# A running sum of squares on VectorE: fewer sums over the partitions in thirteen norms

## The chip, the cores and the metric

The kernel runs on one core of a Trainium2 chip. The metric is the device time of one launch in microseconds (us). TensorE is called PE here, VectorE DVE and ScalarE ACT, as in the profile; SP issues the loads.

## The reference

256 tokens of width 1024 go through two blocks of two layers each. The first block has a gated linear attention layer and a sliding-window attention layer, each followed by a product-key expert layer (PEER); the second has an mLSTM layer and a latent attention layer (MLA), each followed by a squared-ReLU FFN. Every sublayer starts from an RMS norm, and in the second block its output is normed too before it is added:

```python
def rms_norm(x, g):
    xf = x.astype(jnp.float32)
    y = xf * lax.rsqrt(jnp.mean(xf * xf, axis=-1, keepdims=True) + EPS)
    return (y * g.astype(jnp.float32)).astype(x.dtype)

def modulate_2(h, shift, scale):
    return h * (1 + scale[:, None, :]) + shift[:, None, :]
...
        h = modulate_2(rms_norm(x, norm_g[layer, 0]), sh1, sc1)
        ...
        x = x + g1[:, None, :] * rms_norm(y, norm_g[layer, 1])
        h = modulate_2(rms_norm(x, norm_g[layer, 2]), sh2, sc2)
        y = sq_relu_mlp(h, ffn_w1[layer], ffn_w2[layer])
        x = x + g2[:, None, :] * rms_norm(y, norm_g[layer, 3])
```

What matters here is the mean of squares over the 1024 columns of each token.

## The kernel before

Activations lie transposed: the 1024 columns are eight tiles of 128 partitions, and the 256 tokens lie along the free dimension. A sum over the columns is therefore a sum over eight tiles and over the partitions of each. ACT squares a tile (`Stats.add`); DVE adds two squares (`Stats.pairs`); and PE sums over the partitions by a matmul with a matrix of ones, which accumulates in one PSUM region and leaves the sum on every partition (`Stats.sums`). ACT then makes the reciprocal root as Ln and Exp (`rstd`, lines 422 and 423).

Before, the squares of tiles 0 and 1, 2 and 3, 4 and 5 are added in pairs, and tiles 6 and 7 stand alone: five sums. `pairs(2)` is called behind every odd tile and takes up squares that lie at least two tiles back, so the pair (0, 1) is added after tile 3, (2, 3) after tile 5, (4, 5) after tile 7. `total` gives out first the sums that are ready, in their order, then takes up the rest.

The weights come as a stream of chunks of 128x1024 in fp32. Each is split by ACT into a high part (`whi`, line 304) and by DVE into the rest (`wlo`, line 312), and every product is made of three matmuls in fp32r: high by high, high by low, low by high. The order of the instructions on each engine is written out by hand (`manual_schedule`); semaphores follow from the tiles.

Thirteen norms have eight tiles, and they stand in four kinds of places:

- one at the very start (`rstd` of the first stage);
- five in `add_gated`, at the end of the two attention layers and the two PEER layers of the first block: as each pair of accumulators is finished, DVE updates two tiles of x, ACT makes the high part of the next matmul's operand (`xah`) and the square, DVE the low part (`xal`). The last of these places makes two norms at once, the second with a tag of its own and five buffers instead of six;
- four in `add_sandwich`, at the end of each sublayer of the second block: the squares are those of the accumulators; once the sums are done, `ry` is made, and y, x and the next operand follow from it (`fold`, `refresh`);
- three in `fold`, on the x that `refresh` makes two tiles at a time.

For the gated norms and the folds the sums are not made at once: the next stage's first matmuls (`first_linears`, on the operand before the norm's factor, which is applied later) run over the tiles as they come, and PE is given the sums ahead of its last chunk. There are also a norm over two tiles and one over three, both in the MLA layer.

Of the kernel before, what the change touches and what calls it, by code (L numbers as in the profile page):

```python
# [277 lines left out]
class Stream:  # L278
# [4 lines left out]
    def __init__(self, k, dram):  # L283
        self.k, self.nc, self.dram = k, k.nc, dram
        self.off = [0]
        for w in WIDTHS:
            self.off.append(self.off[-1] + 128 * w)
        self.raw, self.hi, self.lo = {}, {}, {}
        self.nd = self.nh = self.nl = self.at = 0
# [84 lines left out]
class Stats:  # L374


    def __init__(self, k, pool, dim, n, dst=None, tag="", ss=None, bufs=6):
        self.bufs = bufs
        self.k, self.pool, self.dim, self.n, self.dst, self.tag = k, pool, dim, n, dst, tag
        self.seen, self.squares, self.ready, self.first = 0, deque(), deque(), ss is None  # L380
        self.ss = k.pw([128, T]) if ss is None else ss
# [7 lines left out]
    def pairs(self, lag=0):  # L389

        while self.squares and self.squares[0][0] + lag < self.seen:
            i, q = self.squares[0]
            if i % 2 == 0 and i + 2 < self.n:
                if i + 1 + lag >= self.seen:
                    return
                self.squares.popleft()
                i, p = self.squares[0]
                self.k.nc.vector.tensor_add(p, p, q)
                q = p
            self.squares.popleft()  # L400
            self.ready.append((i, q))

    def sums(self):
# [1617 lines left out]
```

## Time and profile before

| | before |
|---|---|
| median of 3 runs | 2526.88 us (2524.39 to 2527.84) |
| profiled execution | 2536.26 us, span 2534.5 us |
| PE busy | 2463.7 us (97%) |
| DVE busy | 2093.1 us (83%) |
| ACT busy | 1608.4 us (63%) |
| mean granted clock of PE | 0.993 |

The span runs from the first to the last instruction of the profiled execution. Busy shares are means over the whole span; a place where an engine waits is only seen in the timeline around it.

### The profile page before, as it was taken

What the parts mean: (1) busy time and instruction counts of PE and PEld (TensorE: products, weight loads), DVE (VectorE), ACT (ScalarE), POOL (GpSimd) and SP (SyncE); (2) the same over time, 40 slices, a digit from 0 to 9 for tenths busy, and PEclk for the clock granted to TensorE, in tenths of its full rate; (3) what the DMA queues carried; (4) which work ended last, traced back from release to release, by engine and by line L of the source; (5) the groups of instructions that cost most, each with busy time, mean ns of one, the idle gap of its engine ahead of it and who ended that gap; (6) DMA issues with size and microseconds to landing.
All of it is one profiled execution on the core that took longest, in us unless ns stands there. A gap on an engine that the chain in (4) does not pass through costs nothing.

```text
span 2534.5 us, 52041 instructions
## 1 busy us (share of the span) xinstructions
PE 2463.7 (97%) x20262; PEld 2407.0 (95%) x20262; DVE 2093.1 (83%) x4203; ACT 1608.4 (63%) x3208; POOL 12.4 (0%) x21
## 2 busy tenths in 40 slices
PE   8899999999999999999999999999999999989998
PEld 6799999999999998899999999999998899989998
DVE  8889988998788888699989997787887776786754
ACT  5664459997555545764469996444447666567654
POOL 0000000000000000000000000000000000000000
PEclk9999999999999999999999999999999999999999
DMA  8755554444888884245554445888885547934564
GB/s 324 269 173 184 190 184 150 150 142 148 310 300 313 316 313 161 93 151 192 188 177 144 147 145 198 305 299 301 303 306 183 195 163 262 330 135 130 159 200 142
DMA packets 149174, 537.08 MB, mean 212 GB/s; under 512 B 16560, under 2 KB 18736, under 8 KB 148928
## 3 DMA queue, kind: packets, MB, share of 16 engines
q1 hardware_dynamic: 148640, 533.23, 60.3%
q8 instruction: 159, 2.61, 0.4%
q14 instruction: 87, 0.71, 0.1%
q10 hardware_dynamic: 288, 0.52, 0.1%
HBM read 532.64 MB, written 1.05 MB: 211 GB/s over the span
## 4 chain that ended last, share of the span: by engine, by line
PE 83%; DVE 8%; ACT 5%; DMA 2%; issue 2%; SPq 0%; DVEq 0%; ACTq 0%
PE w L567 12%; PE w L569 12%; PE w L568 12%; PE acc L568 12%; PE acc L569 12%; PE acc L567 12%; PE acc L1345 4%; DVE wlo L312 3%; ACT whi L304 2%; DMA wraw<-in_weights_dram 2%; DVE mraw L650 1%; PE acc L588 1%; PE w L588 1%; PE w L406 1%; PE w L1375 1%
## 5 line engine op out<-in xcount | busy, mean ns | idle before, releaser
L304 ACT CAST whi<-wraw 128x1024 fp32r<-128x1024 f32 x785 | 818.4, 1047 | 684.1 <-PE acc L568 359.3
L312 DVE TENSOR_TENSOR wlo<-wraw,whi 128x1024 fp32r<-128x1024 f32 x785 | 955.2, 1220 | 333.3 <-ACT whi L304 319.8
L567 PE MATMUL w<-hh,whi 128*128 128x256 f32 x2664 | 759.0, 285 | 1.0 <-ACT vz L1475 0.5
L569 PE MATMUL w<-hh,wlo 128*128 128x256 f32 x2664 | 743.3, 279 | 3.1 <-DVE wlo L312 2.9
L568 PE MATMUL w<-hl,whi 128*128 128x256 f32 x2664 | 743.0, 279 | 0.0
L567 PE MATMUL acc<-Wh,whi 128*128 128x256 f32 x2048 | 570.7, 279 | 3.7 <-ACT Wh L762 3.7
L568 PE MATMUL acc<-Wl,whi 128*128 128x256 f32 x2048 | 571.2, 279 | 2.7 <-DVE Wl L763 2.6
L569 PE MATMUL acc<-Wh,wlo 128*128 128x256 f32 x2048 | 570.4, 279 | 0.0
L569 PEld LDWEIGHTS w<-hh,wlo 128*128 128x128 f32 x2664 | 506.3, 190 | 3.7 <-DVE wlo L312 3.7
L567 PEld LDWEIGHTS w<-hh,whi 128*128 128x128 f32 x2664 | 502.5, 189 | 3.6 <-ACT vz L1475 0.9
L568 PEld LDWEIGHTS w<-hl,whi 128*128 128x128 f32 x2664 | 502.2, 189 | 0.7 <-issue 0.5
L568 PEld LDWEIGHTS acc<-Wl,whi 128*128 128x128 f32 x2048 | 388.8, 190 | 3.8 <-DVE Wl L763 3.7
L567 PEld LDWEIGHTS acc<-Wh,whi 128*128 128x128 f32 x2048 | 384.4, 188 | 4.3 <-ACT Wh L762 4.3
L569 PEld LDWEIGHTS acc<-Wh,wlo 128*128 128x128 f32 x2048 | 384.4, 188 | 0.0
L650 DVE SCALAR_TENSOR_TENSOR mraw<-mraw,cact 128x1024 f32<-128x1024 f32 x224 | 272.6, 1219 | 6.6 <-DMA mraw<-in_mods_dram 4.9
L1361 ACT ACTIVATE o<-o,gT 128x128 f32<-128x128 f32 x384 | 161.1, 486 | 0.0
L567 PE MATMUL acc<-yh,whi 128*128 128x256 f32 x512 | 141.6, 277 | 0.9 <-DVE fc L849 0.9
L569 PE MATMUL acc<-yh,wlo 128*128 128x256 f32 x512 | 141.6, 277 | 0.2
L568 PE MATMUL acc<-yl,whi 128*128 128x256 f32 x512 | 141.4, 276 | 0.0
L1345 PE MATMUL acc<-o,o 128*128 128x128 f32 x1024 | 134.6, 274 | 0.0
L1357 ACT ACTIVATE o<-c_iota,iT 128x128 f32<-128x128 f32 x384 | 125.8, 400 | 0.0
L1345 PEld LDWEIGHTS acc<-o,o 128*128 128x128 f32 x1024 | 124.5, 191 | 0.0
(447 smaller groups left out, 3566.4 us busy)
## 6 DMA issues: line engine op xcount, KB each, us to landing
wraw<-in_weights_dram SPq DMA_DIRECT2D x777, 512.0 KB, 3.6
mraw<-in_mods_dram SPq DMA_DIRECT2D x224, 512.0 KB, 5.3
cact<-in_c_dram SPq DMA_DIRECT2D x5, 512.0 KB, 4.2
wraw<-in_weights_dram SPq DMA_DIRECT2D x4, 384.0 KB, 2.9
x<-in_x_dram SPq DMA_DIRECT2D x2, 512.0 KB, 4.4
wraw<-in_weights_dram SPq DMA_DIRECT2D x4, 192.0 KB, 2.4
out_dram<-x SPq DMA_DIRECT2D x2, 256.0 KB, 2.4
out_dram<-x ACTq DMA_DIRECT2D x2, 256.0 KB, 2.4
```

Source lines behind the costliest of these rows:

```text
L304: self.nc.scalar.copy(t[:, :w], self.raw[i][:, :w])
L312: self.nc.vector.tensor_sub(t[:, :w], self.raw.pop(i)[:, :w], self.hi[i][:, :w].bitcast(F32))
L406: self.k.nc.tensor.matmul(self.ss, self.k.ones, q, start=self.first, stop=i == self.n - 1, skip_group_check=True)
L567: mm(out, lh, rh, start=start, stop=False, skip_group_check=True)
L568: mm(out, lh, rl, start=False, stop=False, skip_group_check=True)
L569: mm(out, ll, rh, start=False, stop=stop, skip_group_check=True)
L588: self.nc.tensor.matmul(outs[j], ws[:, i * 128:(i + 1) * 128], xs[:, k], start=k == 0 and ws is wh and xs is x[0], stop=k == KD - 1 and xs ...
L650: self.nc.vector.scalar_tensor_tensor(t, t, 1.0, self.cact, op0=ALU.mult, op1=ALU.mult, accum_out=self.modc[:, n:n + 1])
L1345: nc.tensor.matmul(banks[(n - 1) % 4][:, u], o1[:, u], o2[:, u], start=True, stop=True)
L1357: nc.scalar.activation(o2[:, u], self.iota, AF.Abs, scale=-1.0, bias=iT[:, 1, t:t + 1])
L1361: nc.scalar.activation(o2[:, u], o2[:, u], AF.Relu, scale=gT[:, 1, t:t + 1], bias=gT[:, 0, t:t + 1])
L1375: nc.tensor.matmul(ps[:, b], q[:, b * 128:(b + 1) * 128], sk[:, i % 2], start=True, stop=True)
```

## The change

For a norm over n tiles, the squares of all but the last two tiles are added up in one running sum, each addition reading the result of the one before; the running sum is given to PE when tile n - 3 is in it. The last two squares are summed on their own, as before. The additions are called from the same places. For eight tiles that is five additions and three sums in place of three and five; for three tiles no addition and three sums, in place of one and two; for two tiles nothing changes.

```diff
     def __init__(self, k, pool, dim, n, dst=None, tag="", ss=None, bufs=6):
-        self.bufs = bufs
+        self.bufs, self.run = bufs, None
...
         while self.squares and self.squares[0][0] + lag < self.seen:
-            i, q = self.squares[0]
-            if i % 2 == 0 and i + 2 < self.n:
-                if i + 1 + lag >= self.seen:
-                    return
-                self.squares.popleft()
-                i, p = self.squares[0]
-                self.k.nc.vector.tensor_add(p, p, q)
-                q = p
-            self.squares.popleft()
+            i, q = self.squares.popleft()
+            if i < self.n - 2:
+                if self.run is not None:
+                    self.k.nc.vector.tensor_add(q, q, self.run)
+                self.run = q
+                if i < self.n - 3:
+                    continue
             self.ready.append((i, q))
```

## Rows read from the trace of the kernel before

**Rows 1.** The page: busy time and share by engine; the chain that ended last

```profile
PE 2463.7 (97%) x20262; PEld 2407.0 (95%) x20262; DVE 2093.1 (83%) x4203; ACT 1608.4 (63%) x3208; POOL 12.4 (0%) x21
...
PE 83%; DVE 8%; ACT 5%; DMA 2%; issue 2%; SPq 0%; DVEq 0%; ACTq 0%
```

**Rows 2.** Tiles of squares, by engine: count, least/median/longest ns, first and last start

```profile
L406 PE MATMUL w<-sq,ones x138: 377/379/795, 6.0 to 2524.1; 128*128 128x256 f32 x138
...
L398 DVE TENSOR_TENSOR sq<-sq x40: 417/421/430, 5.5 to 2522.4; 128x256 f32<-128x256 f32 x40
```

**Rows 3.** Timeline, first gated norm: start and length (us), engine, line, [idle before <-releaser]

```profile
152.60 0.51 ACT L461 ACTIVATE xah<-x,ua 128x256 fp32r<-128x256 f32 x1 [0.30 <-DVE x L780]
...
153.65 0.43 DVE L398 TENSOR_TENSOR sq<-sq 128x256 f32<-128x256 f32 x1
...
153.79 2.32 PE L406 MATMUL w<-sq,ones 128*128 128x256 f32 x10
...
155.17 3.50 DVE L312 TENSOR_TENSOR wlo<-wraw,whi 128x1024 fp32r<-128x1024 f32 x3 [0.62 <-ACT whi L304]
...
159.66 0.74 PE L588 MATMUL acc<-hh,whi 128*128 128x256 f32 x4 [0.29 <-ACT hh L742]
```

**Rows 4.** Timeline, first sandwich (end of the mLSTM layer)

```profile
2043.72 1.23 DVE L312 TENSOR_TENSOR wlo<-wraw,whi 128x1024 fp32r<-128x1024 f32 x1 [0.57 <-ACT whi L304]
...
2044.86 1.09 DVE L398 TENSOR_TENSOR sq<-sq 128x256 f32<-128x256 f32 x3
...
2045.43 2.40 PE L406 MATMUL w<-sq,ones 128*128 128x256 f32 x10 [0.30 <-DVE sq L398]
...
2047.86 0.47 ACT L422 ACTIVATE ry<-w,eps 128x256 f32<-128x256 f32 x1 [0.15 <-PE w L406]
...
2048.82 0.43 DVE L821 TENSOR_TENSOR y<-y,ry 128x256 f32<-128x256 f32 x1 [0.48 <-ACT ry L423]
...
2049.28 0.42 DVE L823 TENSOR_TENSOR x<-x,y 128x256 f32<-128x256 f32 x1
...
2050.30 1.01 PE L588 MATMUL w<-xah,whi 128*128 128x258 f32 x3 [2.47 <-ACT xah L461]
```

**Rows 5.** Timeline, first norm, at the start

```profile
5.99 3.87 PE L406 MATMUL w<-sq,ones 128*128 128x256 f32 x10 [5.99 <-DVE sq L398]
...
11.12 0.47 ACT L422 ACTIVATE r<-w,eps 128x256 f32<-128x256 f32 x1
```

**Rows 6.** Timeline, second sandwich (2233 to 2239) and last one (2521 to 2523)

```profile
2233.13 1.09 DVE L398 TENSOR_TENSOR sq<-sq 128x256 f32<-128x256 f32 x3
...
2233.60 2.42 PE L406 MATMUL w<-sq,ones 128*128 128x256 f32 x10 [0.89 <-DVE sq L398]
...
2238.50 0.62 PE L588 MATMUL acc<-xah,whi 128*128 128x258 f32 x3 [2.47 <-ACT xah L461]
...
2521.03 0.43 DVE L398 TENSOR_TENSOR sq<-sq 128x256 f32<-128x256 f32 x1 [4.54 <-ACT sq L385]
...
2522.18 2.32 PE L406 MATMUL w<-sq,ones 128*128 128x256 f32 x10
```

**Rows 7.** Timeline, first fold (start of the first FFN)

```profile
2059.52 0.42 DVE L398 TENSOR_TENSOR sq<-sq 128x256 f32<-128x256 f32 x1
...
2060.52 2.32 PE L406 MATMUL w<-sq,ones 128*128 128x256 f32 x10
```

**Rows 8.** Timeline, second fold (start of the MLA layer)

```profile
2246.55 2.34 PE L406 MATMUL w<-sq,ones 128*128 128x256 f32 x10
...
2246.85 0.42 DVE L398 TENSOR_TENSOR sq<-sq 128x256 f32<-128x256 f32 x1
...
2248.54 0.59 PE L588 MATMUL acc<-xah,whi 128*128 128x258 f32 x2
```

**Rows 9.** Windows after two sandwiches: busy by engine, granted clock, DMA

```profile
2050.50:2053.50 3.00, 3.00 (x15) 3.00 (x16) 2.79 (x6) 2.72 (x9) 0.00 (x0) 0.50 0.12 48
2238.50:2240.50 2.00, 2.00 (x15) 1.86 (x15) 1.97 (x5) 1.72 (x6) 0.00 (x0) 1.00 0.72 264
```

## The prediction

> **What bounds the kernel now.** I read the page first, for who is late on average, then every place where squares are summed in the timeline, because an average over 2.5 ms says nothing about 13 places of a few microseconds. The page shows TensorE (PE) busy for 97% of the span and 83% of the chain that ended last on it [rows 1]: time taken off PE is worth its full length wherever PE doesn't wait. The groups of the squares' tiles come next [rows 2]. The sums over the partitions are 138 MATMULs at one line, and one call gives two of them, so 69 calls: five for each of 13 norms over eight tiles, two for the two-tile norm, two for the three-tile norm. The 40 DVE additions are three for each of the 13 and one for the three-tile norm. Then the timeline of each place, where the reader is to ask one thing: what does PE wait for just before the sums and just after them?
>
> **What one instruction costs.** Ten sum matmuls back to back take 2.32 us, the last of them 0.38 [rows 2, 3], so their pitch is (2.32 - 0.38) / 9 = 0.216 and a call costs 0.43. Six of them run from first start to last end in 5 x 0.216 + 0.38 = 1.46. A DVE addition lasts 0.42. Three independent ones take 1.09 [rows 4], a pitch of (1.09 - 0.42) / 2 = 0.335. The new additions are not independent: each reads what the one before wrote. The nearest row of that kind is the multiply of y at 2048.82 and the addition that reads it at 2049.28, same shape and engine: a pitch of 0.46 [rows 4]. I take 0.46 for the chain and keep 0.335 as the lower end. The Trainium skill (VectorE: DVE Perf Modes, "The DRAIN you can't avoid") says that a DVE instruction starts only when the pipeline has emptied, and that a semaphore between two of them costs nothing extra; by that a chain would cost what independent additions cost, and the sum would be that of the first rival below. The rows above differ from it by 0.125 an instruction.
>
> **What the change moves.** For eight tiles five serial additions replace three independent ones, and six matmuls replace ten. Calls of `pairs` with lag 2 stay where they are: one addition after tile 3 (as now), two after tile 5 (one now), two after tile 7 (one now). The three-tile norm loses its addition and goes from two sums to three. In all PE loses 13 x 2 - 1 = 25 calls, 25 x 0.43 = 10.8 us. DVE gains 25 additions. But the order of the sums is fixed: PE takes the running sum first, and that is now the tile that is ready last of the six; before, PE had two finished pairs to chew on while DVE made the third. So each place is worked out by itself.
>
> *First norm (start).* The sums end at 9.86 (5.99 + 3.87), and its Ln starts at 11.12 [rows 5]. The first addition, 0.42 long and done just before 5.99, starts near 5.5; five chained ones end at 5.5 + 4 x 0.46 + 0.42 = 7.8, and six matmuls at the 0.39 that each of the ten takes there, waits included, end near 10.2. Hidden: 0.
>
> *Four sandwiches* (end of each mixer and FFN of the second block). PE has nothing else to do: sums, then Ln and Exp, y, x, the split, and only then PE again [rows 4]. In the first, DVE comes out of the 1.23 us `wlo` only at 2044.86. The chain ends at 2044.86 + 4 x 0.46 + 0.42 = 2047.12; PE starts 0.05 later (the gap between an addition's end, 2233.13 + 0.42, and its sum at 2233.60 [rows 6]) and ends at 2047.17 + 1.46 = 2048.63, against 2045.43 + 2.40 = 2047.83: **+0.80**. Behind the additions on DVE wait three evacuations of y, a `wlo` and a gain; they end about 0.75 later (a delay of 5 x 0.46 - 1.09 - 0.46), covered by the Ln and Exp. The second: 2233.13 + 2.26 + 0.05 + 1.46 = 2236.90 against 2233.60 + 2.42 = 2236.02: **+0.88**. The third has the first's pattern: +0.80. In the last DVE is idle, the additions start at 2521.03 while PE still accumulates, and the chain ends at 2523.29, the sums at 2524.80 against 2522.18 + 2.32 = 2524.50 [rows 6]: **+0.30**. Together +2.78, and no matmul saved there is worth anything.
>
> *Five gated norms* (in the next stage's first matmuls). PE runs through; but ACT waits for DVE's x (0.30), then come the casts, three `wlo` on DVE from 155.17 to 158.67, the normed tile, and PE waits 0.29 for it at 159.66 [rows 3]. So DVE and ACT set this stage's end, and the extra addition after tile 5 sits ahead of x of tile 6: **+0.46**. The extra one after tile 7 is hidden in DVE's wait for the casts (0.62). The 0.86 saved on PE goes into waiting: the last pair, added at 153.65, becomes a running sum at 153.65 + 0.92 + 0.42 + 0.05 = 155.04, 1.25 after PE comes for it, so PE is 0.39 later too, which the 0.46 covers. Three places: +1.38. The fourth place holds two norms at once, two extra additions ahead of the same x: +0.92. Together +2.30.
>
> *Three folds.* In the first the run of PE isn't broken and the sums stand in it. The last pair now starts at 2059.52; with one more addition after tile 5 and one after tile 7 the running sum is there at 2059.52 + 0.92 + 0.42 + 0.05 = 2060.91, 0.39 after PE comes for it at 2060.52 [rows 7]; PE then has four matmuls less: 0.39 - 0.86 = **-0.47**. The third fold has the same pattern: -0.47. In the second, three outputs bring PE to the sums earlier: 2246.55, when the last pair is only begun at 2246.85 [rows 8]. The running sum is there at 2246.85 + 0.92 + 0.47 = 2248.24; PE now takes 1.99 from the first sum to its next matmul at 2248.54, of which nine pitches are 1.94, so with six it is 5 x 0.216 + 0.03 = 1.11: 2249.35, **+0.81**. Together -0.13.
>
> *Two and three tiles.* The first unchanged; the second one sum more in PE's stream, +0.43 (the removed addition was off the path).
>
> **Sum without the clock:** 2.78 + 2.30 - 0.13 + 0.43 = **+5.4 us**.
>
> **The clock.** After the wait of 2.47 us in the first sandwich the granted clock is 0.50, that is 1.2 GHz, for the following 3 us; after the same wait of 2.47 in the second it is 1.00, 2.4 GHz [rows 6, 9], as three matmuls in 0.62 there and 1.01 here show [rows 4, 6]. So one such wait is a toss-up now. After the change each sandwich has two waits with 1.46 us of work between: some 2 us for the running sum, then 2.47 as now. The Trainium skill (TensorE: Matmul & The Clock Gate, "HAM oscillation — how this bites in real kernels") warns of this pattern, bursts between idle gaps; the trace bears it out in one of the two. Price of one more fall, from rows: 3.2 us (2050.30 to about 2053.5) at half speed, 1.6, if PE alone set the pace. If the fall comes before the sums they take 6 x 0.216 = 1.3 more, on the path, in three sandwiches 3.9. Bounds 0 and 1.6 + 3.9 = 5.5. I take 1.2, near the lower end, since the rows show a fall as likely as none after the longer of the two waits.
>
> **The forecast: +6.6 us.** The profiled execution took 2536.26 (span 2534.5 and 1.8 around it), 9.4 above the median 2526.88; I add the sum to the median: **2533.5**, own range 2530.9 to 2535.9.
>
> **Rivals.**
> *A chained addition costs what an independent one does* (0.335). For: all DVE rows back to back have that pitch; against: the y and x rows. Five additions then take 1.76 instead of 2.26: the first three sandwiches +0.30, +0.38, +0.30, the last -0.13 (there I let the last addition wait for its square, which as now comes no earlier than about 2522.4), gated 5 x 0.335 = 1.68, folds -0.72 twice and +0.56, three-tile +0.43: **+2.1**, 2529.0 without a fall of the clock.
> *The matmuls saved inside PE's stream count in full* (faster). Eight norms stand in it: 8 x 0.86 = 6.9 less, 0.43 more, sandwiches neutral: **-6.5**, 2520.4. It needs the additions hidden: DVE must have slack after tiles 5 and 7, the running sum ready before PE comes. For: DVE is idle 17% of the span [rows 1], and two folds come within 0.4 of it. Against: at the gated norms ACT and PE are seen waiting for DVE. It decides where PE's wait at 159.66 comes from: if that tile isn't held by DVE's x, the 0.46 isn't paid and the 0.86 is gained.
> *The clock falls at each longer wait:* 5.4 + 5.5 = **+10.9**, 2537.8. For: the longer idle time; against: the second sandwich.
>
> **How the numbers follow.** Forecast 0.50, cheap chain 0.22, saved matmuls 0.10, clock 0.18. 0.2% (5.05 us) is about what a measurement of this kernel can tell from no change. Slower by over that: 0.40 of the forecast's 0.50 (its range starts at +4.0) and the clock's 0.18: 0.58. Within: the other 0.10 and 0.22: 0.32. Faster 0.10. The range takes in the cheap chain and the falling clock with 0.7 for how runs differ above it, and 2.5 below the cheap chain for places where a delay is lost again: 2526.5 to 2538.5; the saved matmuls lie outside.
>
> **What would show it.** 88 sum MATMULs and 65 additions; additions after tile 7 of the first sandwich at a pitch of 0.46 (0.335 would be the cheap chain) and PE idle some 2 us before its sums, which end 0.8 later after the last accumulation than now; ACT's wait for x of tile 6 in the gated norms grown by 0.46, PE's wait of 1.25 for the running sum there, and the normed tile's matmul 0.46 later after the last accumulation; fold sums that wait for DVE; the granted clock in and after the three waits. Wrong it would be if the gated norms' next stages came no later, or if a stall is absorbed by a later wait, which would take the total under 0.2%.

## The result, and the profile after

The changed kernel took 2539.5 us in the median of 21 runs (2528.45 to 2563.63), the kernel before 2527.84 in 21 runs beside them (2518.64 to 2550.49): ratio 1.0058, 95% interval 1.004 to 1.0077, that is 10 to 19.5 us more. The fastest run of each differ by 9.8 us. The profiled executions go the other way: 2530.90 us (span 2529.1) after, 2536.26 (span 2534.5) before. Both facts have to be explained, so one pair of profiles isn't enough here.

The page of the changed kernel: busy time by engine, and the chain that ended last by engine [rows 1].

```profile
PE 2443.7 (97%) x20212; PEld 2387.3 (94%) x20212; DVE 2101.9 (83%) x4228; ACT 1609.3 (64%) x3208; POOL 12.4 (0%) x21
...
PE 83%; DVE 8%; ACT 5%; DMA 2%; issue 1%; SPq 0%; DVEq 0%; ACTq 0%
```

The tiles of squares [rows 2], with what the engines waited for on their account:

```profile
L404 PE MATMUL w<-sq,ones x88: 377/379/794, 8.1 to 2518.8; 128*128 128x256 f32 x88
L395 DVE TENSOR_TENSOR sq<-sq x65: 411/424/427, 5.5 to 2517.1; 128x256 f32<-128x256 f32 x65
...
  DVE sq L395: 41.1, 17
```

88 matmuls and 65 additions, as the change says. The last line is idle time that an addition ended, 41.1 us in 17 waits (PE and its weight loads counted apart); in the kernel before it was 15.6 in 8. PE's busy time fell by 20.0 us, of which 50 matmuls of 0.216 are only 10.8; the other 9 has another source, which the first experiments show.

The timeline of the changed kernel, in order of time: the first gated norm (152 to 162, [rows 3]), the first sandwich (2033 to 2041, [rows 4]), the first fold (2049 to 2052, [rows 7]), the second sandwich and fold (2222 to 2240, [rows 6, 8]), the third sandwich, and the last one (2515 to 2519, [rows 6]).

```profile
152.85 0.88 DVE L395 TENSOR_TENSOR sq<-sq 128x256 f32<-128x256 f32 x2
...
154.15 0.51 ACT L459 ACTIVATE xah<-x,ua 128x256 fp32r<-128x256 f32 x1 [0.77 <-DVE x L778]
...
156.24 1.53 PE L404 MATMUL w<-sq,ones 128*128 128x256 f32 x6 [1.24 <-DVE sq L395]
...
156.72 3.50 DVE L312 TENSOR_TENSOR wlo<-wraw,whi 128x1024 fp32r<-128x1024 f32 x3 [0.16 <-ACT whi L304]
...
161.21 0.74 PE L586 MATMUL acc<-hh,whi 128*128 128x256 f32 x4 [0.27 <-ACT hh L740]
...
2033.50 2.54 DVE L395 TENSOR_TENSOR sq<-sq 128x256 f32<-128x256 f32 x5
...
2036.18 1.53 PE L404 MATMUL w<-sq,ones 128*128 128x256 f32 x6 [2.38 <-DVE sq L395]
...
2037.75 0.47 ACT L420 ACTIVATE ry<-w,eps 128x256 f32<-128x256 f32 x1 [1.22 <-PE w L404]
...
2038.71 0.42 DVE L819 TENSOR_TENSOR y<-y,ry 128x256 f32<-128x256 f32 x1 [0.28 <-ACT ry L421]
...
2040.18 0.63 PE L586 MATMUL w<-xah,whi 128*128 128x258 f32 x3 [2.47 <-ACT xah L459]
...
2050.80 1.56 PE L404 MATMUL w<-sq,ones 128*128 128x256 f32 x6 [1.57 <-DVE sq L395]
...
2222.65 2.53 DVE L395 TENSOR_TENSOR sq<-sq 128x256 f32<-128x256 f32 x5
...
2225.23 1.56 PE L404 MATMUL w<-sq,ones 128*128 128x256 f32 x6 [3.00 <-DVE sq L395]
...
2229.26 0.63 PE L586 MATMUL acc<-xah,whi 128*128 128x258 f32 x3 [2.47 <-ACT xah L459]
...
2239.01 1.56 PE L404 MATMUL w<-sq,ones 128*128 128x256 f32 x6 [1.07 <-DVE sq L395]
...
2326.12 2.54 DVE L395 TENSOR_TENSOR sq<-sq 128x256 f32<-128x256 f32 x5
...
2328.80 2.60 PE L404 MATMUL w<-sq,ones 128*128 128x256 f32 x6 [2.00 <-DVE sq L395]
...
2333.88 1.01 PE L586 MATMUL w<-xah,whi 128*128 128x258 f32 x3 [2.47 <-ACT xah L459]
...
2515.00 2.55 DVE L395 TENSOR_TENSOR sq<-sq 128x256 f32<-128x256 f32 x5 [4.54 <-ACT sq L385]
...
2517.60 1.56 PE L404 MATMUL w<-sq,ones 128*128 128x256 f32 x6 [1.29 <-DVE sq L395]
```

The reader is to see three things. In the sandwiches and the first two folds PE now has a wait of 1.1 to 3.0 us for DVE's running sum. In the gated norm ACT's wait for x grew from 0.30 to 0.77. And six sums that took 1.53 in the first sandwich took 2.60 in the third; the windows over the two say why (stretch, length, PE's busy time and matmuls, granted clock, DMA share, GB/s):

```profile
2328.80:2330.90 2.10, 2.10 (x6) 0.57 0.13 51
2036.20:2037.70 1.50, 1.50 (x6) 1.00 0.11 44
```

In the third the granted clock was 0.57 in the mean, so most of the stretch ran at 1.2 GHz; in the first it was 1.00, 2.4 GHz.

**One measure for the sandwiches.** From the start of the first addition to the start of the first product matmul behind the sums, both read from the timeline (first sandwich before: 2050.30 - 2044.86 = 5.44; after: 2040.18 - 2033.50 = 6.68). It leaves out when DVE comes to the additions, which differs from execution to execution. The experiments below are in the table too; "h" marks sums that ran in a stretch of halved clock.

| kernel | 1st | 2nd | 3rd |
|---|---|---|---|
| before | 5.44 | 5.37 | 5.43 |
| copy_before | 5.43 | 5.37 | 5.43 |
| changed | 6.68 | 6.61 | 7.76 h |
| copy_after | 6.69 | 6.62 | 7.11 h |
| sandwich_only | 8.05 h | 8.00 h | 6.69 |
| run_last | 6.31 | 6.39 | 6.31 |
| run_last_wlo | 5.76 | 6.29 h | 5.76 |
| tree | 6.04 | 7.05 h | 6.04 |
| adds_more | 5.79 | 5.86 | 5.78 |
| sums_less | 5.17 | 5.17 | 5.25 |
| fewer | 5.41 | 5.49 | 5.50 |
| gated_late | 8.05 h | 7.42 h | 6.69 |
| after_busy | 6.62 | 6.63 | 6.63 |
| before_busy | 5.44 | 5.38 | 5.43 |

### The profile page after: what moved, and what is told of

Its sections match the earlier page's. It is cut to its first block, busy times and chain, and to the rows that moved or that the text cites. A ratio compares the mean times of both kernels' runs of the same rounds, so it can differ in the third digit from the quotient of the medians.

```text
span 2529.1 us, 51992 instructions
## 1 busy us (share of the span) xinstructions
PE 2443.7 (97%) x20212; PEld 2387.3 (94%) x20212; DVE 2101.9 (83%) x4228; ACT 1609.3 (64%) x3208; POOL 12.4 (0%) x21
## 4 chain that ended last, share of the span: by engine, by line
PE 83%; DVE 8%; ACT 5%; DMA 2%; issue 1%; SPq 0%; DVEq 0%; ACTq 0%
PE w L565 12%; PE w L567 12%; PE w L566 12%; PE acc L566 12%; PE acc L567 12%; PE acc L565 12%; PE acc L1343 5%; DVE wlo L312 2%; ACT whi L304 2%; DMA wraw<-in_weights_dram 2%; DVE mraw L648 1%; PE acc L586 1%; PE w L586 1%; DVE sq L395 1%; PE w L404 1%
```

## The experiments

**copy_before** and **copy_after**: the two kernels once more, with no edit.

> The kernel before once more, unchanged; it shows what one program's executions differ by. Two theories of the measured +14.7 us. Serial sum: the running sum, taken first by PE, delays thirteen places; place by place, from the two profiles, that is +8 to +9 us (sandwiches +1.2, +1.25, +2.4, +0.7, gated norms +0.5 three times and +0.8, folds -0.4, +0.9, 0, three-tile norm +0.3), and the rest is chance. Pace: in long stretches of 128x256 matmuls PE starts one every 113.3 or every 117.8 ns, and which of the two is not chance but tied to the program, so that the changed one gets the slow pace more often. If chance, this copy's profile has the two paces in other stretches than the first profile (1546 to 1906 us was slow there), and its ratio is within 0.3% of 1; if tied, the stretch from 1546 to 1906 us is slow again and the executions agree within a few microseconds.

> The changed kernel once more, unchanged. Serial sum: every place costs what it did in the first profile of it, within 0.2 us, but for places where the clock is halved; ratio 1.003 to 1.006. Pace tied to the program: the stretches that were slow in its first profile (1105 to 1303 us among them) are slow again, those fast there fast again, and the ratio is again near 1.006 with at least 6 us that no place explains.

Measured: copy_before 2525.9 us against 2530.74 for the kernel before beside it (ratio 0.9992, 0.9968 to 1.0016), copy_after 2540.97 against the same 2530.74 (1.0053, 1.0022 to 1.0083). In both, the runs of one program lie 23 to 32 us apart. The windows over two long stretches show what moves them: PE is busy all the time at a granted clock of 1.00, and still runs a different number of matmuls. Each line is the stretch, its length, PE's busy time and matmuls, clock, DMA share, GB/s. The kernel before, first profile:

```profile
1600.00:1850.00 250.00, 250.00 (x2125) 1.00 0.83 301
```

copy_before:

```profile
200.00:360.00 160.00, 160.00 (x1361) 1.00 0.57 188
400.00:600.00 200.00, 200.00 (x1768) 1.00 0.44 146
...
780.00:960.00 180.00, 180.00 (x1591) 1.00 0.87 315
...
1600.00:1850.00 250.00, 250.00 (x2208) 1.00 0.87 312
```

The changed kernel, first profile:

```profile
1600.00:1850.00 250.00, 250.00 (x2208) 1.00 0.88 314
```

sandwich_only (below):

```profile
780.00:960.00 180.00, 180.00 (x1531) 1.00 0.85 302
...
1600.00:1850.00 250.00, 250.00 (x2125) 1.00 0.84 303
```

PE has two paces for the same matmuls: 250 / 2125 = 117.6 ns each or 250 / 2208 = 113.2. The first profile of before had the slow one in this stretch, its copy the fast one; sandwich_only had it slow also from 780 to 960, where both profiles of before and both of the changed kernel were fast. Over the 14 profiles of this study the stretch was slow in five, of kernels of both kinds. At 4.4 ns a matmul and some 3100 matmuls it is worth 13.6 us, and it explains why the first pair of profiles went the wrong way. So the pace in that stretch is not tied to the program: one program had both. Whether one kernel meets the slow pace more often than another, single profiles can't tell. The copies also give a clean comparison: copy_before, the changed kernel and copy_after had the same paces in all long stretches, with spans of 2519.6, 2529.1 and 2527.6. The change costs **8.0 to 9.5 us** there (one profile of before against two of the changed kernel).

**sandwich_only** and **run_last**

```diff
# sandwich_only: pairs of the kernel before, but in add_sandwich
-    def __init__(self, k, pool, dim, n, dst=None, tag="", ss=None, bufs=6):
+    def __init__(self, k, pool, dim, n, dst=None, tag="", ss=None, bufs=6, old=True):
...
-        st = Stats(self, pool, D, KD, self.late.tile([128, T], F32, name="ry", tag="ry"))
+        st = Stats(self, pool, D, KD, self.late.tile([128, T], F32, name="ry", tag="ry"), old=False)
# run_last: against the changed kernel
-                if i < self.n - 3:
+                if self.n > 3:
                     continue
             self.ready.append((i, q))
+            if i == self.n - 1 and self.n > 3:
+                self.ready.append((self.n, self.run))
...
```

> The running sum in the four sandwiches alone; the pairs of the kernel before at every other norm. Serial sum: the first product matmul behind the sandwiches comes +1.2, +1.25, +1.2 to +2.4 and +0.7 us later after the last accumulation than in the kernel before, every other place stays within 0.1 us: places +4.4 to +5.6 in all, ratio 1.002 with the gated norms' and folds' 3 to 4 us gone. Rival, that the sandwiches cost only what was forecast: +2.8 in all, ratio 1.001. Pace tied to the program: the ratio has nothing to do with these sums and may come out at 1.005 or below 1.

Measured: 2530.41 us, ratio 1.0009 (0.9979 to 1.0039), too wide to decide. The places do: gated norms and folds within 0.1 of the two profiles of before, sandwiches +1.26 at full clock (the third) and +2.6 in the first two, whose sums ran at half clock:

```profile
2052.34 2.54 DVE L407 TENSOR_TENSOR sq<-sq 128x256 f32<-128x256 f32 x5
...
2055.02 2.90 PE L416 MATMUL w<-sq,ones 128*128 128x256 f32 x6 [2.22 <-DVE sq L407]
```

The rival of +2.8 in all falls: 1.26 alone is more than the forecast's 0.80 to 0.88.

> The changed kernel with the running sum given to PE last, behind the squares of tiles 6 and 7. Serial sum: PE sums tiles 6 and 7 while DVE still adds, and after the last addition only two matmuls (0.60 us) stand where six (1.53) stood, so Ln starts 0.9 us sooner in each sandwich: +0.3 against the kernel before in place of +1.2, and the second fold also 0.9 sooner; places +3.9 in place of +8.5. Rival, that what delays the sandwiches is DVE's additional work itself (the evacuations of y queued behind it): the Ln comes 0.9 sooner but the first product matmul behind it does not. Pace tied to the program: ratio anywhere from 0.998 to 1.008, whatever the places do.

Measured: 2535.59 us, 1.0013 (0.9987 to 1.004). Half right: the sandwiches come out at +0.88 to +1.02 in place of +1.25, not at +0.3. First sandwich:

```profile
2036.15 2.54 DVE L395 TENSOR_TENSOR sq<-sq 128x256 f32<-128x256 f32 x5
...
2038.74 0.70 PE L406 MATMUL w<-sq,ones 128*128 128x256 f32 x2 [0.47 <-DVE sq L395]
...
2039.48 0.47 ACT L422 ACTIVATE ry<-w,eps 128x256 f32<-128x256 f32 x1 [0.29 <-PE w L406]
2039.78 1.22 DVE L312 TENSOR_TENSOR wlo<-wraw,whi 128x1024 fp32r<-128x1024 f32 x1
2039.98 0.42 ACT L423 ACTIVATE ry<-ry 128x256 f32<-128x256 f32 x1
2040.99 0.42 DVE L821 TENSOR_TENSOR y<-y,ry 128x256 f32<-128x256 f32 x1
```

Ln starts 3.33 behind the first addition (2039.48 - 2036.15) where it started 4.25 behind it in the changed kernel, 0.9 sooner; but the root, ready at 2040.40, lies until DVE has finished its additions, three evacuations and a `wlo`. The rival named for it holds: behind PE's wait stands DVE's queue.

**run_last_wlo**: that `wlo` moved out of the way.

```diff
             nc.vector.tensor_scalar(y[:, d], self.part(acc, d), gg[:, d:d + 1], None, op0=ALU.mult)
-        self.w.prepare()
...
                 self.refresh(s, f.shift)
                 evacuate(5)
+                self.w.prepare()
```

> The kernel with the running sum given to PE last, and the wlo that DVE makes between the sandwich's evacuations and the norm's multiplication moved behind the first tile of x. With the running sum last, Ln started at 3.04 to 3.14 us after the last accumulation in the first and third sandwich, 0.2 to 0.3 behind the kernel before, but the multiplication that reads the root only 1.5 later in place of 0.95. If DVE's queue is what held it: multiplication 0.95 behind Ln again, and the first product matmul at 5.5 to 5.6 in place of 6.0 to 6.1 (first and third sandwich), +0.2 to +0.4 against the kernel before. Rival, ACT or the evacuations hold it: no change.

Measured: the multiplication 0.96 behind Ln, sandwiches +0.33 (first and third; in the second the clock fell); 2537.12 us, ratio 1.0042 (1.0021 to 1.0064).

```profile
2038.73 0.47 ACT L422 ACTIVATE ry<-w,eps 128x256 f32<-128x256 f32 x1 [0.28 <-PE w L406]
...
2039.69 0.42 DVE L820 TENSOR_TENSOR y<-y,ry 128x256 f32<-128x256 f32 x1 [0.49 <-ACT ry L423]
...
2041.16 0.63 PE L588 MATMUL w<-xah,whi 128*128 128x258 f32 x3 [2.47 <-ACT xah L461]
```

DVE's queue is shown to be the next limit of a sandwich. It isn't a gain by the end of the fold: from the last accumulation to the first product behind the fold's sums the three places took 17.76, 18.34 and 17.70, in run_last 17.53, 17.31 and 18.40. The `wlo` now stands ahead of the next tiles, and in the first fold the tile's low part comes so late that PE waits 0.51 for it.

**sums_less** and **adds_more**: one half of the change each.

```diff
# sums_less: against the kernel before
-            self.ready.append((i, q))
+            if self.n != 8 or i not in (5, 6):
+                self.ready.append((i, q))
# adds_more: against the kernel before
                 self.k.nc.vector.tensor_add(p, p, q)
+                if self.n == 8 and i > 1:
+                    self.k.nc.vector.tensor_add(q, p, q)
```

> The kernel before with its additions as they are, but PE sums three of the five: the pair (4, 5) and tile 6 are left out of every eight-tile sum, so the sums are too small. It is the saved matmuls alone. Forecast's reading: nothing in the gated norms (0 within 0.1), since DVE and ACT set their end, -0.87 in each fold (four matmuls of 0.216), and in the sandwiches -0.87 at the Ln but less, about -0.5, at the next product matmul, because DVE is then held by a wlo until 0.4 us after the root is there. Total -4 to -5 us. Rival, saved matmuls count in full: -0.87 at all thirteen places, -11 us, the gated norms included.

> The kernel before with its five sums, and two more additions on DVE in each eight-tile norm, one behind the pair (2, 3) and one behind (4, 5), each reading what the addition ahead of it wrote and writing to a square that nobody reads any more. It is DVE's time alone. Forecast's reading: gated norms +0.46 (twice that where two norms are made), as in the changed kernel, although PE's sums wait for nothing new; folds 0; sandwiches 0 at the sums and at most +0.5 behind them, from the evacuations that stand behind the additions. Total +2.5 to +4.5. Rival, PE's wait for the serial sum is what costs in the gated norms too: 0 there, total under +1.

Measured: sums_less 2524.79 us, 0.9978 (0.9948 to 1.0008); adds_more 2533.15, 1.0011 (0.9982 to 1.0041). Between the same two product matmuls on either side of a single gated norm, sums_less stands 0.01 to 0.04 from before, adds_more +0.48 to +0.51, the changed kernel +0.47 to +0.53. In adds_more PE's sums wait for nothing new, and ACT waits the same 0.77:

```profile
153.14 0.51 ACT L463 ACTIVATE xah<-x,ua 128x256 fp32r<-128x256 f32 x1 [0.77 <-DVE x L782]
```

So in the gated norms four matmuls are worth nothing and an addition on DVE its full pitch: the forecast's reading, and "saved matmuls count in full" falls. In the folds four matmuls less gave 0.7 to 0.9, near the 0.87 expected. In the sandwiches sums_less gave only 0.2, for ACT and DVE come no sooner, and the additions alone cost 0.35 to 0.5.

**tree**: the five additions of the sandwiches in another order.

```diff
+                if self.tree is not None:
+                    self.tree.append(q)
+                    if i % 2:
+                        add(q, q, self.tree[-2])
+                    if i == self.n - 3:
+                        add(self.tree[3], self.tree[3], self.tree[1])
+                        add(q, q, self.tree[3])
...
```

> The changed kernel, but in the four sandwiches the same five additions are made as a tree: (0, 1), (2, 3), (4, 5), then (2, 3) with (0, 1), then (4, 5) with both. Same count, same sums, one or two steps in which an addition reads what the one just ahead wrote, in place of four. If the reading of a result just written is what stretches a step from 0.335 to 0.53: the five take 1.9 to 2.0 us in place of 2.54, and the first product matmul behind a sandwich comes 0.4 to 0.6 sooner than in the changed kernel (+0.7 against the kernel before in place of +1.3, at full clock). Rival, five additions cost the same in any order: no change at the sandwiches.

Measured: 2536.59 us, 1.0009 (0.9977 to 1.004); the third sandwich:

```profile
2340.47 1.09 DVE L398 TENSOR_TENSOR sq<-sq 128x256 f32<-128x256 f32 x3
2341.47 0.42 DVE L400 TENSOR_TENSOR sq<-sq 128x256 f32<-128x256 f32 x1
2341.93 0.42 DVE L401 TENSOR_TENSOR sq<-sq 128x256 f32<-128x256 f32 x1
...
2342.49 1.53 PE L412 MATMUL w<-sq,ones 128*128 128x256 f32 x6 [1.46 <-DVE sq L401]
```

Five additions in 2341.93 + 0.42 - 2340.47 = 1.88 in place of 2.54, and the first and third sandwich at +0.61 in place of +1.25: half of the sandwich's price is the serial order, not the count.

**gated_late**: the additional addition behind x of tiles 6 and 7.

```diff
-                st.pairs(2)
+                st.pairs(3 if d == 5 else 2)
```

> The changed kernel, but after tile 5 only one addition is made (as in the kernel before) and after tile 7 three, so that the additional one stands behind DVE's x of tiles 6 and 7 and not ahead of them; same count, same sums. If its place ahead of x is what costs the gated norms 0.46: they come out at 0 to +0.2 against the kernel before, and the place of two norms at +0.2 or less in place of +0.9 to +1.1, although PE now waits longer for the running sum. Rival, the count of additions is what costs, wherever they stand: +0.46 again. Folds, where DVE's order changes too: first fold -0.8 as before or up to 0.4 worse. Sandwiches unchanged by it at +1.25.

Measured: single gated norms +0.23 to +0.27 in place of +0.47 to +0.53, the place of two norms still +1.1. That is a miss: 0 to +0.2 was expected, and at most +0.2 at the place of two. Its place ahead of x accounts for half of the single norms' price. The other half, 0.22 in the first gated norm, is how much later DVE's three `wlo` start: the cast comes when it came in the kernel before, but the `wlo`, which waited 0.62 for it there [rows 3] and 0.16 in the changed kernel (row 156.72), now stand behind three additions with no idle time left:

```profile
154.95 1.34 DVE L395 TENSOR_TENSOR sq<-sq 128x256 f32<-128x256 f32 x3
...
156.68 3.49 DVE L312 TENSOR_TENSOR wlo<-wraw,whi 128x1024 fp32r<-128x1024 f32 x3
```

2541.06 us, ratio 1.0063 (1.0042 to 1.0085), with halved clock in the sums of two sandwiches.

**after_busy** and **before_busy**: PE kept busy in the sandwiches.

```diff
         self.accumulate(acc, chunk, x, False, True, each)
+        for i in range(5):   # after_busy: into st.ss, which the sums overwrite
+            nc.tensor.matmul(st.ss, self.ones, self.x[:, 7], start=True, stop=True, skip_group_check=True)
         st.total()
+        p = self.pw([128, T])   # before_busy: here in its place
+        for i in range(5):
+            nc.tensor.matmul(p, self.ones, self.x[:, 7], start=True, stop=True, skip_group_check=True)
```

> The changed kernel with five more matmuls calls (ten matmuls, 2.2 us) on PE in each sandwich between the last accumulation and the sums, on data that is ready and with a result that the sums overwrite: PE is not idle while DVE makes the running sum. If the idle time is what lets the clock fall: six sums in 1.53 to 1.56 in all sandwiches, and the third at +1.25 like the others in place of +1.7 to +2.2. Rival, the fall is chance and has nothing to do with the wait: one or more of the three sandwiches with sums of 1.9 to 2.9, as in 5 of the 12 with a wait of over 2 us so far. The wait for the running sum itself stays, since DVE sets it.

> The kernel before with five more matmul calls (2.2 us) on PE behind the sums of each sandwich, on data that is ready and into a region that nobody reads, so that the wait of 2.47 us for the next operand is filled. If that wait lets the clock fall: the first three product matmuls take 0.62 behind every sandwich (1.01 where the clock was halved), no stretch of halved clock starts in the 4 us behind the wait, worth up to 1 us a sandwich where it fell. Rival: PE behind these waits is held by DVE anyway, and nothing changes but a matmul delayed by the filler. Ratio 0.997 to 1.001 either way.

Measured: after_busy 2544.25 us, 1.0059 (1.0032 to 1.0087); six sums in 1.56 in all sandwiches, and all at +1.2, the third too:

```profile
2353.99 2.32 PE L803 MATMUL w<-x,ones 128*128 128x256 f32 x10
2356.17 1.56 PE L404 MATMUL w<-sq,ones 128*128 128x256 f32 x6
```

The filler keeps the clock up in front of these sums, but it doesn't make the kernel faster. The three places with their folds took 19.16, 18.91 and 18.16, 56.2 in all, against 56.4 and 55.4 in the two profiles of the changed kernel, and in the second fold, where PE has no filler and waits for the running sum, the sums ran at half clock.

before_busy 2526.16 us, 0.9999 (0.9975 to 1.0023): behind the filler the wait is 0.31 in place of 2.47, three products take 0.62 to 0.63 behind each of the three, and no stretch of halved clock starts there. In the two profiles of before one did behind four of six such waits.

```profile
2041.07 2.32 PE L807 MATMUL w<-x,ones 128*128 128x256 f32 x10
...
2043.70 0.62 PE L588 MATMUL w<-xah,whi 128*128 128x258 f32 x3 [0.31 <-ACT xah L461]
```

Over all profiles of first to third sandwiches: behind an idle wait of 1.5 to 3.0 us for a running sum or tree the sums met a halved clock in 7 of 15 (changed, copy_after, sandwich_only, tree, gated_late); with the pairs of before, where PE waits 0.9 at most, in 0 of 18; with PE kept busy in 0 of 3, which by itself would also come out so by chance one time in seven. run_last and run_last_wlo, with two waits of 0.5 to 1.4 each, met it in 1 of 6. So the fall goes with the idle time; in which place it comes differs even between executions of one program: behind the 2.47 waits it was the first and third sandwich in before, the first and second in copy_before. In the table the seven cost 0.4 to 1.4 each against sums at full clock, 7.5 in all, a mean of 0.5 over the 15.

**fewer**: meant to beat both.

```diff
# sandwiches and second fold: tile 6 is added to tile 7 as well
-            if i % 2 == 0 and i + 2 < self.n:
+            if i % 2 == 0 and i + (2 if self.mode == 0 else 1) < self.n:
...
# first and third fold: running sum, given last (mode 1)
```

> A version meant to beat both: the kernel before with its gated norms and first norm as they are; in the sandwiches and the second fold four pairs, four sums (tile 6 added to tile 7: one more independent addition, one sum less); in the first and third fold the running sum, given to PE last. From the rows: sandwiches -0.43 at the Ln, and at the next product matmul -0.1 to -0.4, as DVE's queue allows; first and third fold -0.87 each, as the changed kernel with the running sum last showed; second fold -0.4. Total -2.5 to -3.7 us, ratio 0.9987, which is under what the times can tell; the places in the profile decide. Rival: the fourth addition holds up the sandwiches' evacuations, and they come out at 0 or above: total -1.5.

Measured: 2529.16 us, 0.9995 (0.9966 to 1.0023). First and third fold about -0.9 each; the sandwiches 0 to +0.1, as the rival had it, since Ln then waits for ACT's evacuations and the multiplication for DVE; the second fold lost some 2.4, from 2.21 to 4.61 between the products on either side of its sums. There the fourth addition stands behind two `wlo` on DVE, and PE waits 2.61 for it:

```profile
2249.23 2.36 DVE L312 TENSOR_TENSOR wlo<-wraw,whi 128x1024 fp32r<-128x1024 f32 x2 [0.73 <-ACT whi L304]
...
2251.51 0.42 DVE L409 TENSOR_TENSOR sq<-sq 128x256 f32<-128x256 f32 x1
...
2251.98 0.98 PE L417 MATMUL w<-sq,ones 128*128 128x256 f32 x2 [2.61 <-DVE sq L409]
```

The granted clock was 1.00 up to there (2248.0 to 2251.8) and fell only behind the wait (0.55 from 2252.0 to 2254.5). It is the fault of the change once more: a saved matmul paid for with an addition that comes late. No version here is measurably faster than the kernel before.

## Why the prediction went wrong

The sign and the places were right, the size was not: +6.6 forecast, 8.0 to 9.5 at equal paces, and a median 11.7 higher. (Of the 6.0 between the 2533.5 forecast and the 2539.5 measured, 1.0 is the base: the kernel before came out at 2527.84 beside it, not at 2526.88.) PE runs the same 20,124 other matmuls in the same order in every run, so the cost of a place can be read between the same two of them. By the forecast's own terms; measured is the mean of the two profiles of the changed kernel less the mean of the two of before, between the same matmuls on either side, the fold with its sandwich:

| term | forecast | measured |
|---|---|---|
| first norm | 0 | 0 (Ln at 11.02, before 11.12) |
| three single gated norms | +1.38 | +1.5 |
| place of two norms | +0.92 | +0.9 |
| first sandwich and fold | +0.33 | +0.85 |
| second sandwich and fold | +1.69 | +2.2 |
| third sandwich and fold | +0.33 | +2.4 |
| last sandwich | +0.30 | +0.70 (end of its sums; +0.6 at the end of the span) |
| three-tile norm | +0.43 | +0.45 (against copy_before) |
| sum | +5.4 | +9.0 |
| clock | +1.2 | in the rows above |

**The step that failed: "Four sandwiches", +2.78.** Each was mis-sized by 0.4. "I take 0.46 for the chain": the two-addition runs bear that out (0.88 for two, so a pitch of 0.46), but in the sandwiches five take 2.54, a pitch of (2.54 - 0.42) / 4 = 0.53, 0.28 more in all. There each addition waits for the one before on DVE and for a square of ACT's that no earlier instruction waited for; in the gated norms the square is long known to be there. In tree and adds_more, in the sandwiches, a chained addition that reads no new square takes 0.45 to 0.46 from start to start (2341.93 - 2341.47 in tree), which fits; that this is the reason was not tried by itself. PE starts 0.14 behind the chain (2036.18 - 2036.04), not 0.05, and six sums take 1.53, not 1.46. The last could have been seen: ten sums took 2.40 behind a wait in [rows 4], not the 2.32 that the 1.46 comes from. Together 0.44: +1.24 where 0.80 was forecast, and +1.25 measured; with +0.70 for the last, four sandwiches cost +4.45 at full clock where +2.78 was forecast.

The cheap-chain rival falls: the rows here show 0.335 between independent additions and 0.46 or 0.53 between chained ones, and in tree the order alone is worth 0.66. The Trainium skill (VectorE: DVE Perf Modes, "The DRAIN you can't avoid") says of copies that a semaphore between two DVE instructions costs nothing extra; for additions that read the one ahead, what the forecast drew from it does not hold, and the measurement decides.

**Folds, "-0.47".** That step took from the profile that PE would wait 0.39 for the running sum in the first fold. PE came that late there because its clock was halved in front of the place [rows 9]. In the changed kernel it was not: the products between sandwich and fold took 8.75 in place of 10.1 to 10.2, and PE came to the sums sooner and waited 1.57 (row 2050.80). From the last product ahead of these sums to the first behind them it took 3.07 in both profiles of the changed kernel, 2.09 in both of before: the fold itself cost +0.98 where -0.47 was forecast. That sandwich and fold together cost only 0.85 is the clock that stayed up between them, which the forecast didn't foresee. In tree's third sandwich, at full clock throughout, the fold cost 0.9 more on top of 0.61: first product behind the fold's sums 17.58 us behind the last accumulation, 16.05 in copy_before. A wait read from a stretch with a fallen clock is too short.

**The clock, +1.2.** The mechanism was right, and the mean about right: 0.5 a sandwich over 15 waits, 1.5 for three; the 1.2 was chosen, not worked out. In both profiles of the changed kernel the fall struck the third sandwich, but it is not what makes up that row's +2.4. From the last accumulation to the first product behind the fold's sums, gated_late took 18.23 there at full clock, the changed kernel 19.62 and 18.65, copy_before 16.05 at full clock and before 17.40 with half clock behind the sandwich. At full clock on both sides the place costs +2.2, sandwich and fold; the fall adds 0.4 to 1.4 to the changed kernel, and the kernel before has a fall of its own. (The additions of gated_late's fold are placed a little differently; PE waits 1.93 for them there, 1.86 in the first fold of the changed kernel.)

**A rival that came near.** The rival of a clock that falls at each longer wait (+10.9) lies nearest to the medians. That is luck: the sums met a fallen clock in 7 of 15, not in all, and its other terms are the forecast's, too small by the sandwiches' 1.7.

**What was right.** Nothing at the start; the gated norms, by mechanism and size, with DVE and ACT as the limit; the second fold's direction (+2.2 less 1.25 is +0.9, forecast +0.81); the extra addition after tile 7 hidden in DVE's wait for the casts (0.62 less 0.46, and 0.16 is left in row 156.72); that DVE's evacuations hide behind the root, with 0.28 left (row 2038.71), and no further, as run_last shows. "Saved matmuls" is right in the folds alone, where PE doesn't wait.

**What stays open.** The medians differ by 11.7 and 10.2 us, the first ratio's interval begins at 10 (copy_after's at 5.6), and the places give 8.0 to 9.5. That the changed kernel meets the slow pace more often could fill the gap, but the profiles don't show it, nor could so few; the cause of the gap stays open. The forecast had no term for the two paces, which alone move an execution by more than the whole change.

## What to carry to other kernels

Count a saved instruction only where its engine doesn't wait on both sides of it: here 25 sum calls came off PE, and no row of the table came out sooner, since PE then waited for DVE, the engine that got the work. A serial sum that is consumed first puts its whole latency ahead of the consumer; give it last, or make it a tree, and look at what is queued behind it on the producer. Read waits from an execution with full clock, and take a second profile of the unchanged kernel before explaining a difference of under 1%.

## What the runs showed of the hardware

- PE runs long stretches of 128x256 fp32r matmuls with weight loads at 117.6 or 113.2 ns each, at a granted clock of 1.00 in both. From 200 to 360 us it was slow and from 400 to 600 fast in every profile; from 1600 to 1850 it differed between two executions of one program, from 780 to 960 between single profiles of different kernels. What sets it is not known.
- DVE additions of 128x256 in fp32: 0.335 from start to start when independent, 0.46 when one reads the result of the one ahead, 0.53 in the sandwiches' chain, where each also reads a new square of ACT's.
- After 1.5 to 3.0 us of idle PE between short bursts the next sums met the 1.2 GHz clock in 7 of 15 cases, after 0.9 at most in 0 of 18. With ten matmuls on unused data in the wait it was 0 of 3, too few to call it prevented, and the kernel was no faster for it.
